# Other orders and buffer homes at eleven places of a hybrid decoder block

## The chip, the cores and the metric

The kernel runs on one core of a Trainium2 chip. A core has five engines that work side by side, each with its own stream of instructions: TensorE (PE, matrix products, with PEld for its weight loads), VectorE (DVE), ScalarE (ACT), GpSimd (POOL) and SyncE (SP), which here only issues transfers. Transfers run on 16 DMA engines, fed by the queues of the engines that issue them. Data lives in HBM (called DRAM tiles in the code), in SBUF, where the engines work, and in eight PSUM banks, into which PE accumulates. The metric is the device time of one execution in microseconds (us); lower is better.

## The reference, cut to what matters

One decoder block on a sequence of 1024 tokens with 1024 channels, in float32:

```python
mod = silu(c) @ w_ada + b_ada                       # six rows: shift, scale, gate, twice
h = rms_norm(x, pre_norm1_w) * (1 + sc1) + sh1
z, xbc, dt_raw, q, k, v, gates = split(h @ w_in)    # 1024, 1536, 16, 3 x 1024, 2048 columns
xbc = silu(causal_dwconv(xbc, 4 taps))              # Mamba-2 branch, 16 heads, chunks of 128
y_ssd = rms_norm(ssd(xbc, softplus(dt_raw + dt_bias), a_log, d_skip) * silu(z))
y_att = differential attention of q, k (rotary), v  # 8 pairs of heads, causal
merged = sigmoid(g_ssd) * (y_ssd @ w_ssd_o) + sigmoid(g_att) * (y_att @ w_attn_o)
x = x + g1 * rms_norm(merged @ w_out, post_norm1_w)
h2 = rms_norm(x, pre_norm2_w) * (1 + sc2) + sh2
u_gate, u_val = split(causal_dwconv(h2 @ w_up, 3 taps))      # 2 x 2816 channels
x = x + g2 * rms_norm((gelu(u_gate) * u_val) @ w_down, post_norm2_w)
```

## The kernel before, in words

**Products.** Nearly every product is made in three passes. An operand is split into a high part, rounded to `fp32r`, and a low part, the rest (`split`, L92: an ACT copy, L93, and a DVE difference, L94); PE adds high by high, high by low and low by high (`mm3`, L115 to 117). So a weight block costs one load of 512 KB, one copy on ACT and one difference on DVE before PE can use it. The two products of the feed-forward part, `w_up` and `w_down`, are made by a Strassen-like scheme of seven products instead of eight, on sums and differences of quarter blocks.

**Homes.** SBUF outside the weight rings is cut into 43 slots of 4 KB a partition (`Slots`, L35). `get` takes the slot that was freed longest ago, `get_last` the one freed last, `put` gives slots back. A tile that takes a slot waits for the last user of its previous tile. The weight rings `wraw` (3 buffers), `whi` and `wlo` (4 each) turn by themselves.

**Order.** Each engine runs its own instructions in order. Inside `tc.manual_schedule(engines=...)` the engines named keep the order in which the code issues; elsewhere a planner sets each engine's order by its own estimate of costs. SP's stream matters too: a store that waits for its data holds up the loads issued behind it.

**Stages,** in the order of the program, with the lines that the change touches:
- *Modulation and `h`* (L137 to 322).
- *Projection to `xbc`* (L429 to 461): twelve blocks, only PE in written order. Each block is followed by a convolution on ACT and DVE in `cu` (L440 to 447; L445 is the tap that reads the bank) and by three or four steps of the remaining modulation rows: `ada_load` (512 KB into one of four `adas`), `ada_sum` (DVE, L387), and once for eight of them `ada_row` (L389), with two matmuls (L398), two or three DVE operations and three small transfers. `down_sums(k)` (L411) makes the sums of quarter blocks of `w_down` that its seven products need: two loads into `wdr`, four subtractions in `wds` on POOL, two stores to `wtd` (L422), 11 rounds in all. Their homes are taken at L407 and L408.
- *z* (L478 to 498): three column groups of eight token blocks, six rounds of `down_sums` among them. Behind the loop stand the *decays* (L501 to 541): softplus and cumulative sums (L521, the matmuls at L523, the transposes L539 to `acT`) for the chunks.
- *Chunks of the SSD branch* (L543 to 765), with the `v` projection as filler for PE: `v_stream` (L596) yields after each contraction step; `split_v` (L583) puts four half operations for each weight tile in the background list `bg`, of which `run_bg` takes some at each turn.
- *Gates* (L769 to 779), the last five rounds of `down_sums`, *q and k* (L837 to 862: rotary positions, `store_qk` with 16 transfers a block, `load_y` and `turn_y` for the transposed `y`), *`w_ssd_o`* (L865 to 889; SP and PE in written order; `gths` at L869 and L876).
- *Attention* (L1114 to 1193): PE, DVE and ACT in written order; `probs` (L1044 to 1058) is the softmax of an item, `norm_o` (L1082) ends a group of rows, `att_split` (L1168) brings the result back as operands `oT`.
- *`w_attn_o`* (L1227 to 1250), by the planner: eight blocks `ao`, the split of the second half of `w_out` (`wo[1]`), and `early_sums` (L1211), four DVE sums (L1216 to 1219) on `w_up` for the first three up blocks.
- *Mix and norm* (L1391 to 1540): from here PE, DVE, ACT and POOL are in written order. `load_res` picks a pair of the banks m0 to m3 for each row block; `mix_square`, `mix_end` (L1415, `xr` scaled at L1427), `first_half`, `turn` (transposes L1452) make the feed-forward operand `HB`. `w_load` and `w_split` bring the up weights.
- *Up pairs* (L1542 to 1729): 22 of them, a gate block and a value block each; a pair takes seven steps of 12 matmuls (L1344 to 1346) into its banks X, Y and Z. Between steps the banks are copied to `evs` or added (L1712 and its neighbours), which I call passage copies. `w_ahead` splits the weights some steps on; `convs` says after which step the convolution, Gelu and product (`up_conv`, L1352) and the sums of the finished pair (`up_gsum`, L1375) are issued. Pairs 0 and 1 run together, in an order that is written out, and pair 2 starts it off into the loop.
- *Down* (L1731 to 1836): `left_part` loads the result back through two `gst` buffers (L1762) and splits it, `right_part` brings `w_down`; seven products (`downs`) of six double steps (11 contraction blocks) by four token blocks, 3 or 6 matmuls each (L1813 to 1815); then the norm and the output.

The down stage's homes (`gst`, and `gop` for two whole left operands, 24 tiles) are taken behind L1737, where the up stage gives its own back:

```python
1735    for n, _ in order:
1736        SL.put(*HB[n])
1737    SL.put(*sab, *hls, *cgv[0], *cgv[1], *evs, *ug, uv, *gsum)
```

Of the kernel before, what the change touches and what calls it, by code (L numbers as in the profile page):

```python
# [17 lines left out]
P = 128  # L18
# [43 lines left out]
def kernel(ctx: ExitStack, tc: tile.TileContext, a: dict, out: bass.AP, dbg=None):  # L62
# [398 lines left out]
    SL.put(*cu, *accr, *adas, nrow, brow)  # L461
    xsT, BT, CT = xbcT[:8], xbcT[8:10], xbcT[10:12]
# [14 lines left out]
    n_ev, n_dn = 0, 0  # L477
    for c0, wdt in ((0, 346), (346, 346), (692, 348)):  # L478
        wz = [load_moving(a["w_zdt"], 2 * kp, 2, c0, wdt, f"wz{c0}_{kp}") for kp in range(4)]
        for i in range(8):  # L480
# [16 lines left out]
            SP.dma_start(zd[i][:, c0 + lo - NH : c0 + lo - NH + n], e[:, 1, :n])  # L497
    SL.put(*ev, *wdr, *wds)


    CH = 8 * NH  # L501
    aexp = const("aexp", [P, NH])
    f = lambda t: t.rearrange("p c h -> p (c h)")
    t0 = f(sp0_)
    t1 = sp1_
    x_ = f(dtr)
    V.scalar_tensor_tensor(t0, x_, -1.0, x_, op0=ALU.mult, op1=ALU.min)
    A.activation(t0, t0, AF.Exp)
    V.tensor_scalar(t1, t0, 2.0, None, op0=ALU.add)
    V.reciprocal(t1, t1)  # L510
    V.tensor_tensor(t0, t0, t1, op=ALU.mult)
    V.tensor_tensor(t1, t0, t0, op=ALU.mult)
    dtf = f(dt)
    V.tensor_scalar(dtf, t1, 2.0 / 15, 2.0 / 13, op0=ALU.mult, op1=ALU.add)
    for m in (11, 9, 7, 5, 3, 1):
        V.tensor_tensor(dtf, dtf, t1, op=ALU.mult)
        V.tensor_scalar(dtf, dtf, 2.0 / m, None, op0=ALU.add)
    V.tensor_tensor(dtf, dtf, t0, op=ALU.mult)
    V.scalar_tensor_tensor(dtf, x_, 0.0, dtf, op0=ALU.max, op1=ALU.add)
    A.activation(aexp, rows[:, R_AL : R_AL + NH], AF.Exp)  # L520
    V.scalar_tensor_tensor(la, dt, -1.0, aexp[:, None, :].broadcast_to([P, 8, NH]), op0=ALU.mult, op1=ALU.mult)  # L521
    pa = ps_wa("acum_ps")
    T.matmul(pa[:, :CH], tri, f(la), start=True, stop=True)  # L523
    T.matmul(pa[:, CH : 2 * CH], ones, f(la), start=True, stop=True)
    V.tensor_copy(f(acum), pa[:, :CH])
    A.activation(f(ea), f(acum), AF.Exp)
    A.activation(f(cd), pa[:, CH : 2 * CH], AF.Exp)
    V.tensor_tensor(f(dte), pa[:, CH : 2 * CH], f(acum), op=ALU.subtract)
    A.activation(f(dte), f(dte), AF.Exp)
    hi_r = hi_t  # L530
    V.tensor_copy(hi_r, acum)
    V.tensor_copy(acx[:, :, :NH], hi_r.bitcast(F32))
    V.tensor_tensor(acx[:, :, NH:], acum, hi_r.bitcast(F32), op=ALU.subtract)
    acT = SL.get("acT", F32R, (P, S))
    V.memset(acT.bitcast(F32), 0.0)
    for half in range(2):
        pt = ps_wa(f"acT_ps{half}")
        for q in range(4):
            T.transpose(pt[:32, q * P : (q + 1) * P], acx[:, 4 * half + q, :], ident)  # L539
        V.tensor_copy(acT[:32, half * HALF : (half + 1) * HALF], pt[:32, :])  # L540
    SL.put(hi_t)
    dump("dt", dtf)
    dump("acum", f(acum))  # L543
# [39 lines left out]
    def split_v(vh, kp, raw):  # L583
# [7 lines left out]
        def low(k):  # L591
            return lambda: V.tensor_tensor(lo[:, k], raw[:, k], hi[:, k].bitcast(F32), op=ALU.subtract)
# [882 lines left out]
    with tc.manual_schedule(engines={EN.PE, EN.DVE, EN.Activation, EN.Pool}):  # L1475
# [114 lines left out]
        for m in range(2):  # L1590
            w_split(m, 4)
# [309 lines left out]
```

## Time and profile before

| | us |
|---|---|
| runs | 1933.61, 1944.59, 1941.97 |
| their median | 1941.97 |
| the profiled execution | 1938.42 |
| its span, first to last instruction | 1936.6 |
| PE busy in the span | 1871.4 (97%) |
| DVE busy | 1204.9 (62%) |
| ACT busy | 852.2 (44%) |
| POOL busy | 212.2 (11%) |
| mean granted TensorE clock | 0.994 of full speed |

How the rows shown below are read. A row such as `PE upx L1344 <- ACT evs L1712: 4.8, 2, 3.5` is one of the waits: instructions of PE at line 1344 with the tile `upx` stood 4.8 us in all, 2 times, the longest 3.5, for what ACT did to `evs` at line 1712. A row of windows begins with the stretch in us from the start of the span, then its length, and the busy time and number of instructions of PE, PEld, DVE, ACT and POOL, and ends with the granted clock, the share of DMA busy time and GB/s. A row of the timeline is start, duration, engine, line, operation, out<-in with shapes, count, and in square brackets the idle time before it and what ended it. A row of a group (line, engine, operation, tiles) has busy time and mean ns after the first bar, and the engine's idle time in front of it, with what ended it, after the second. A row of transfers has queue, number, size and the median us from issue to landing.

### The profile page before, as it was taken

The page shows a single profiled execution, that of the slowest core. Times are in us where ns is not written, and L with a number is a line of the kernel's source. Part 1 is how long each engine was busy: PE and PEld are TensorE (multiplying, and loading weights), DVE is VectorE, ACT ScalarE, POOL GpSimd, SP SyncE. Part 2 cuts the span into 40 slices and gives each one's busy share as a digit, 9 for nine tenths or more (in the row PEclk, how much of TensorE's full clock was granted, in tenths as well). Part 3 has the DMA queues.
Part 4 walks back from the last instruction along what each step waited for, and adds up shares of the span by engine and source line. Part 5 has one row for each costly group of instructions (what it writes and reads, how often), then busy time and mean ns, then how long its engine had stood idle before and what let it go on. Part 6 is the DMA issues. An engine that isn't in the chain of part 4 may idle for free.

```text
span 1936.6 us, 24512 instructions
## 1 busy us (share of the span) xinstructions
PE 1871.4 (97%) x9128; PEld 1557.7 (80%) x9128; DVE 1204.9 (62%) x1819; ACT 852.2 (44%) x1634; POOL 212.2 (11%) x214
## 2 busy tenths in 40 slices
PE   6999999999999999999999999999999999989998
PEld 4777898878887788888888787877788888878886
DVE  6968333565235227767766553367988888885545
ACT  5522224555223015665565522455554545455432
POOL 0253001453350000000000100000000000000001
PEclk9999999999999999999999999999999999999999
DMA  9876132233766646565651865122322322377754
GB/s 304 286 285 220 48 117 86 71 109 112 266 200 171 224 152 186 148 190 155 167 153 56 273 238 185 44 76 76 141 93 103 115 98 92 115 245 265 234 157 158
DMA packets 135821, 310.52 MB, mean 160 GB/s; under 512 B 16779, under 2 KB 48139, under 8 KB 135702
## 3 DMA queue, kind: packets, MB, share of 16 engines
q1 hardware_dynamic: 128406, 282.74, 45.6%
q0 software_dynamic: 7296, 26.22, 3.8%
q8 instruction: 72, 1.18, 0.3%
q14 instruction: 47, 0.39, 0.1%
HBM read 219.49 MB, written 89.41 MB: 160 GB/s over the span
## 4 chain that ended last, share of the span: by engine, by line
PE 78%; DVE 10%; DMA 5%; ACT 4%; issue 3%; SPq 1%; POOL 0%; POOLq 0%; DVEq 0%; ACTq 0%
PE upx L1345 3%; PE upx L1346 3%; PE upx L1344 3%; PE o L1078 3%; PE dx L1814 2%; PE dx L1815 2%; PE dx L1813 2%; PE upy L1345 2%; PE upy L1346 2%; PE upy L1344 2%; PE v L606 2%; PE v L607 2%; PE dy L1815 2%; PE dy L1813 2%; PE z L116 2%
## 5 line engine op out<-in xcount | busy, mean ns | idle before, releaser
L1344 PE MATMUL upx<-t,wu_t 128*128 128x512 f32 x264 | 104.0, 394 | 4.8 <-ACT evs L1712 4.8
L1345 PE MATMUL upx<-t,wu_t 128*128 128x512 f32 x264 | 103.7, 393 | 1.9 <-DVE t L1459 1.9
L1346 PE MATMUL upx<-t,wu_t 128*128 128x512 f32 x264 | 103.2, 391 | 0.0
L1066 ACT COPY aT<-at 128x512 f32<-128x512 f32 (+2 forms) x96 | 46.1, 480 | 110.0 <-PE at L1065 110.0
L1318 ACT ACTIVATE wu_t<-sab 128x512 fp32r<-128x512 f32 x57 | 34.0, 626 | 122.5 <-DVE sab L1335 122.5
L94 DVE TENSOR_TENSOR g_lo<-gst,g_hi 128x1024 fp32r<-128x1024 f32 (+1 forms) x42 | 47.5, 1134 | 56.9 <-ACT g_hi L93 56.9
L1078 PEld LDWEIGHTS o<-vt,aT 128*128 128x128 f32 x576 | 75.1, 192 | 9.5 <-ACT aT L1066 5.3
L1078 PE MATMUL o<-vt,aT 128*128 128x128 f32 x576 | 81.0, 277 | 0.2
L142 POOL TENSOR_TENSOR rsf<-rsf,nhalf 128x1 f32<-128x1 f32 x8 | 5.6, 703 | 639.6 <-DVE rsf L141 636.9
L93 ACT ACTIVATE g_hi<-gst 128x1024 fp32r<-128x1024 f32 (+1 forms) x42 | 41.5, 989 | 77.3 <-DMA gst<-gld_s 36.6
L115 PE MATMUL xbc<-hT,wx_hi 128*128 128x512 f32 x160 | 64.4, 402 | 4.8 <-DVE cu L445 4.8
L1039 DVE TENSOR_REDUCE nmx<-sc 128x1 f32<-128x640 f32 (+3 forms) x64 | 65.6, 1025 | 2.2
L142 POOL TENSOR_TENSOR sqt<-sqt,nhalf 128x4 f32<-128x4 f32 x16 | 16.2, 1010 | 443.3 <-DVE sqt L141 443.3
L1019 PE MATMUL sc<-kst,qst 128*128 128x512 f32 (+2 forms) x192 | 63.7, 340 | 0.0
L1344 PEld LDWEIGHTS upx<-t,wu_t 128*128 128x128 f32 x264 | 49.9, 189 | 16.6 <-ACT evs L1712 5.6
L1020 PE MATMUL sc<-klo,qst 128*128 128x512 f32 (+2 forms) x192 | 63.2, 346 | 0.0
L116 PE MATMUL xbc<-hT,wx_hi 128*128 128x512 f32 x160 | 63.0, 394 | 0.0
L117 PE MATMUL xbc<-hT,wx_lo 128*128 128x512 f32 x160 | 62.8, 393 | 0.0
L115 PE MATMUL z<-wz_hi,hT 128*128 128x346 f32 (+1 forms) x192 | 61.8, 324 | 0.0
L116 PE MATMUL z<-wz_lo,hT 128*128 128x346 f32 (+1 forms) x192 | 61.8, 322 | 0.0
L117 PE MATMUL z<-wz_hi,hT 128*128 128x346 f32 (+1 forms) x192 | 61.5, 320 | 0.0
L1345 PEld LDWEIGHTS upx<-t,wu_t 128*128 128x128 f32 x264 | 50.0, 189 | 13.2 <-DVE t L1459 2.9
(444 smaller groups left out, 5858.8 us busy)
## 6 DMA issues: line engine op xcount, KB each, us to landing
adas<-in_w_ada SPq DMA_DIRECT2D x32, 512.0 KB, 5.3
wdr<-in_w_down POOLq DMA_DIRECT2D x22, 512.0 KB, 7.2
wtd<-wds POOLq DMA_DIRECT2D x22, 512.0 KB, 4.7
wuf<-in_w_up SPq DMA_DIRECT2D x22, 512.0 KB, 3.5
gld_s<-gsum SPq DMA_DIRECT2D x22, 512.0 KB, 2.9
gst<-gld_s SPq DMA_DIRECT2D x20, 512.0 KB, 5.0
wdt_raw<-wtd SPq DMA_DIRECT2D x20, 512.0 KB, 4.6
wuv<-in_w_up SPq DMA_DIRECT2D x19, 512.0 KB, 3.9
```

Of the source, the lines that this page charges most:

```text
L115: T.matmul(ps, lh, rh, start=(i == 0), stop=False)
L116: T.matmul(ps, lh, rl, start=False, stop=False)
L117: T.matmul(ps, ll, rh, start=False, stop=(i == n - 1))
L1019: T.matmul(sc[:, n0:n1], qs_[s][:, tsl], ks_[s][:, n0:n1], start=True, stop=False)
L1020: T.matmul(sc[:, n0:n1], qs_[s][:, tsl], kl[s][:, n0:n1], start=False, stop=True)
L1039: V.reduce_max(nmx[:, bq, s : s + 1], sc[:, :L], axis=AX.X, negate=True)
L1078: T.matmul(po_of[j, grp][:, qi, :], at[:, k, :], vt[j % 2][:, kt, :], start=(kt == 0), stop=(kt == i))
L1344: T.matmul(out_, wh, xh_, start=(k == 0 and first), stop=False, skip_group_check=not first)
L1345: T.matmul(out_, wh, xl_, start=False, stop=False, skip_group_check=not first)
L1346: T.matmul(out_, wl, xh_, start=False, stop=(k == end), skip_group_check=not first)
L1813: T.matmul(bank[q], gh[:, kk, tsl], wh, start=(k == 0 and not more), stop=False, skip_group_check=more)
L1815: T.matmul(bank[q], gl[:, kk, tsl], wh, start=False, stop=(k == KF - 1), skip_group_check=more)
```

## The change

Eleven places are changed; no product is added or taken away.

1. *Projection.* In `ada_row` the three small transfers go out on POOL's queue instead of SP's. `wdr` and `wds` are taken after the block loop has given back `cu`, `accr`, `adas`, `nrow` and `brow`, instead of before it.
2. *Decays.* They become a function, issued after the first third of z. `acT` and `aexp` are taken before the z loop.
3. *`w_v`, second half.* Each tile is split by one ACT and one DVE operation that are issued in the stream itself, at steps 2 to 7 of its last block of the first half and 0 and 1 of the next.
4. *`y`.* `load_y(1)` goes from the head of the fifth q/k block to the fourth, before its `store_qk`. The first `gths` load comes inside the written order of SP.
5. *Attention.* POOL is added to the engines in written order.
6. *`w_attn_o`.* `early_sums` at blocks 1, 2 and 6 instead of 0, 1 and 6; the `wo[1]` tiles at 3 to 6 instead of 2 to 5.
7. *Mix.* Row blocks 0 and 1 use the banks wa, wb and wc instead of m0 to m3.
8. *First up weights.* `w_split(0, 1)` and one `w_load` are issued in row block 6 instead of 7, `w_split(1, 0)` in 7 instead of 6.
9. *Pairs 0 to 2.* High parts are issued before passage copies at several places; `high("t1", 0)` two steps up; `w_split(m, 5)` in two pieces; the copy of X of pair 2 later.
10. *The tables of the loop.* Convolutions of pairs 0 and 2 and the sums of pair 1 are issued one step later or split over two steps; at p = 3 and 4 of pair 2 they follow the passage copies and weight splits; at p = 2 the bank sum of pair 2 comes right after the first two.
11. *Down.* `left_part`, `right_part`, the matmuls (`down_mms`) and the first product come into the written order. In the last pair the operands' slots are given back as they are used, `gst` is taken at p = 3, and `left_part(0, ...)` is issued from p = 3 on, `right_part` from p = 5 on. Convolution, Gelu and sums of the last pair (`rest`) are issued within the first product, one group after each double step. `gop` takes its slots one by one; `es` takes them before `evs`, `ug` and the like are given back, `fo` after.

```diff
@@ ada_row
-        SP.dma_start(br, a["b_ada"][0:1, g * D : (g + 1) * D])
+        G.dma_start(br, a["b_ada"][0:1, g * D : (g + 1) * D])
         if g != 3:
-            SP.dma_start(nr, a["norms"][r : r + 1, :])
+            G.dma_start(nr, a["norms"][r : r + 1, :])
...
-        SP.dma_start(rowd[r], br)
+        G.dma_start(rowd[r], br)
     brow = SL.get("brow")
-    wdr = [SL.get_last(f"wdr{i}", F32, (P, 2, HALF)) for i in range(2)]
-    wds = [SL.get_last(f"wds{i}", F32, (P, 2, HALF)) for i in range(2)]
...
     SL.put(*cu, *accr, *adas, nrow, brow)
+    wdr = [SL.get_last(f"wdr{i}", F32, (P, 2, HALF)) for i in range(2)]
+    wds = [SL.get_last(f"wds{i}", F32, (P, 2, HALF)) for i in range(2)]
@@ z; decays() holds what stood behind the loop
+        if c0 == 0:
+            decays()
@@ split_v, v_stream
-        later(("wv", vh, kp), high(0), high(1), low(0), low(1))
+        if vh == 0:
+            later(("wv", vh, kp), high(0), high(1), low(0), low(1))
+            return
+        finished.add(("wv", vh, kp))
+        A.activation(hi, raw, AF.Copy)
+        return lambda: V.tensor_tensor(lo, raw, hi.bitcast(F32), op=ALU.subtract)
...
-                    if vh == 0 and i == 7 and k % 2 == 1:
-                        split_v(1, k // 2, v_raw.pop(0))
-                        if k == 1:
-                            v_raw.append(fetch_v(1, 3))
+                    if (vh == 0 and i == 7 and k > 1) or (vh == 1 and i == 0 and k < 2):
+                        if k % 2 == 0:
+                            v_low.append(split_v(1, (k // 2 - 1) % 4, v_raw.pop(0)))
+                        else:
+                            v_low.pop()()
+                            if k == 3:
+                                v_raw.append(fetch_v(1, 3))
@@ q and k, w_ssd_o
-            load_y(1)
...
+            if n == 3:
+                load_y(1)
...
-    SP.dma_start(gths[0], gsd[0])
     with tc.manual_schedule(engines={EN.SP, EN.PE}):
+        SP.dma_start(gths[0], gsd[0])
@@ attention, w_attn_o
-    with tc.manual_schedule(engines={mybir.EngineType.PE, mybir.EngineType.DVE, mybir.EngineType.Activation}):
+    with tc.manual_schedule(engines={EN.PE, EN.DVE, EN.Activation, EN.Pool}):
...
-        if j in (0, 1, 6):
-            early_sums(j if j < 2 else 2)
-        if 2 <= j < 6:
-            kp = j - 2
+        if j in (1, 2, 6):
+            early_sums(min(j - 1, 2))
+        if 3 <= j < 7:
+            kp = j - 3
@@ mix and norm
-        pms[i] = [ps_m(2 * (i % 2) + ch, f"mix{i}_{ch}") for ch in range(2)]
+        if i < 2:
+            pms[i] = [(ps_wa, (ps_wb, ps_wc)[i])[ch](f"mix{i}_{ch}") for ch in range(2)]
+        else:
+            pms[i] = [ps_m(2 * (i % 2) + ch, f"mix{i}_{ch}") for ch in range(2)]
...
                     w_split(0, 0)
-                    w_split(1, 0)
-                if i == 7 and n == 1:
                     w_split(0, 1)
                     w_load()
+                if i == 7 and n == 1:
+                    w_split(1, 0)
                     w_split(1, 1)
@@ pairs 0 to 2 (the highs of t3 and b22, w_split(m, 5) move likewise)
+        high("t1", 0, r1s)
         t2_sum(3)
...
-            if k == 1:
-                for m in range(2):
-                    A.copy(ev_of(m, 1), banks[m]["X"])
...
+        t3_sum(3)
+        SL.put(*r1s)
+        for m in range(2):
+            A.copy(ev_of(m, 1), banks[m]["X"])
+        high("t3", 0, hb1)
...
         up_mms(2, 0)
-        A.copy(ev_of(2, 0), banks[2]["X"])
...
             high("t4", k, hb2)
+        A.copy(ev_of(2, 0), banks[2]["X"])
@@ tables
-            (2, 2): ((0, 0), (0, 1)),
+            (2, 2): (),
...
-            (3, 2): ((2, 0),),
-            (3, 3): ((2, 1),),
-            (3, 4): ((2, 2),),
+            (3, 2): (),
+            (3, 3): ((2, 0),),
+            (3, 4): ((2, 1), (2, 2)),
...
-        convs[3, 1] = [(up_gsum, 1, i) for i in range(4)]
+        convs[3, 1] = [(up_gsum, 1, i) for i in range(2)]
+        convs[3, 2] = [(up_gsum, 1, i) for i in range(2, 4)]
...
-                if m == 2 and p in (3, 4):
-                    for f_, *x_ in todo:
-                        f_(*x_)
-                    todo = []
...
-                    if m > 2:
-                        V.tensor_tensor(cg[:, :HALF], bank["Z"], ev_of(m, 0), op=ALU.add)
+                    if m == 2:
+                        up_conv(0, 0)
+                        up_conv(0, 1)
+                    V.tensor_tensor(cg[:, :HALF], bank["Z"], ev_of(m, 0), op=ALU.add)
...
-                    if m == 2:
-                        V.tensor_tensor(cg[:, :HALF], bank["Z"], ev_of(m, 0), op=ALU.add)
@@ last pair and down; left_part and right_part as before, but for gop's slots
+                if m == NPAIR - 1:
+                    SL.put(*HB[order[p][0]])
+                    if p == 3:
+                        SL.put(*sab)
+                        gst = [SL.get_last(f"gst{i}", F32, (P, 2, HALF)) for i in range(2)]
+                    if p >= 3:
+                        left_part(0, p - 3)
+                    if p >= 5:
+                        wd[p - 5] = right_part(0, p - 5)
...
+        rest = [[(up_conv, m, 0), (up_conv, m, 1)], [(up_conv, m, 2), (up_conv, m, 3)], [(up_conv, m, 4), (up_gsum, m, 0), (up_gsum, m, 1)], [(up_gsum, m, 2), (up_gsum, m, 3)]]
+        for kp in range(KP):
+            for q in range(4):
+                down_mms(0, kp, q)
+                if q == 0 and kp + 4 < KP:
+                    left_part(0, kp + 4)
+                elif q == 1 and kp + 2 < KP:
+                    wd[kp + 2] = right_part(0, kp + 2)
+                elif q == 2:
+                    if kp < KP - 1:
+                        left_part(1, kp)
+                    for f_, *x_ in rest[kp] if kp < len(rest) else ():
+                        f_(*x_)
+        left_part(1, KP - 1)
+    es = [SL.get(f"es{i}", F32, (P, 2, HALF)) for i in range(4)]
+    SL.put(*cgv[0], *cgv[1], *evs, *ug, uv, *gsum)
...
-    for kp in range(KP):
-        left_part(0, kp)
```

More of the change, by code (lines that the diff above doesn't have):

```diff
@@ L1595 @@
             both(3, [k])
+        cgv = [[SL.get(f"c{n}{i}") for n in ("g", "v")] for i in range(2)]
+        for k in range(KH):
+            HB["b22"][k] = new_hl(f"b22_{k}")
         for k in range(KH):
@@ L1598 @@
             both(4, [k])
-        cgv = [[SL.get(f"c{n}{i}") for n in ("g", "v")] for i in range(2)]
+        for m in range(2):
+            w_high(m, 5)
+        for k in range(KH):
+            high("b22", k, c22)
         for m in range(2):
@@ new lines, in down_mms @@
+        def down_mms(p, kp, q):
+            rn, bk = downs[p][1:]
+            more = rn in ("t2", "t3", "t4", "b22")
+            o = dbank[bk][q]
+            tsl = slice(q * P, (q + 1) * P)
+            gh, gl = gop[p % 2][kp]
+            for kk in range(min(2, KF - 2 * kp)):
+                k = 2 * kp + kk
+                wh, wl = wd[kp][0][:, kk, :], wd[kp][1][:, kk, :]
+                T.matmul(o, gh[:, kk, tsl], wh, start=(k == 0 and not more), stop=False, skip_group_check=more)
+                T.matmul(o, gh[:, kk, tsl], wl, start=False, stop=False, skip_group_check=more)
+                T.matmul(o, gl[:, kk, tsl], wh, start=False, stop=(k == KF - 1), skip_group_check=more)
@@ L1655, in w_ahead @@
+        wd = {}
         def w_ahead(m, p):
```

211 lines of the change are left out of this document (97 added, 114 removed).

## The prediction, made before the changed kernel ran

> **What bounds the kernel now.** I read the page first: busy time by engine, and the chain that ended last.
>
> ```profile
> PE 1871.4 (97%) x9128; PEld 1557.7 (80%) x9128; DVE 1204.9 (62%) x1819; ACT 852.2 (44%) x1634; POOL 212.2 (11%) x214
> PE 78%; DVE 10%; DMA 5%; ACT 4%; issue 3%; SPq 1%; POOL 0%; POOLq 0%; DVEq 0%; ACTq 0%
> ```
>
> TensorE is the bound nearly everywhere, and the change removes no matmul. It can gain only where PE stands still or runs slowly. So I cut the span into windows. The first number of a row is the window's length, the second PE's busy time, and the granted clock stands before the last two.
>
> ```profile
> 100.00:120.00 20.00, 18.83 (x83) 15.31 (x82) 13.53 (x10) 4.94 (x5) 10.29 (x11) 1.00 0.91 346
> 178.00:200.00 22.00, 18.35 (x71) 14.01 (x70) 14.12 (x14) 5.76 (x6) 0.00 (x0) 0.92 0.19 41
> 314.00:330.00 16.00, 13.02 (x73) 10.82 (x71) 9.25 (x18) 9.13 (x26) 4.29 (x4) 0.89 0.57 191
> 405.00:415.00 10.00, 7.92 (x39) 5.59 (x38) 6.90 (x9) 5.92 (x15) 4.95 (x4) 1.00 0.58 161
> 613.00:650.00 37.00, 34.56 (x166) 27.50 (x165) 10.84 (x14) 8.10 (x11) 0.00 (x0) 1.00 0.62 207
> 1069.00:1077.00 8.00, 5.88 (x28) 4.74 (x27) 4.02 (x8) 2.94 (x5) 2.00 (x4) 0.79 0.94 316
> 1093.00:1110.00 17.00, 14.77 (x58) 10.02 (x58) 9.57 (x13) 8.40 (x13) 0.00 (x0) 1.00 0.90 305
> 1184.00:1190.00 6.00, 4.53 (x20) 3.49 (x19) 4.82 (x7) 2.29 (x3) 0.00 (x0) 1.00 0.87 300
> 1262.00:1290.00 28.00, 26.56 (x128) 21.73 (x127) 17.29 (x29) 15.54 (x34) 3.09 (x5) 1.00 0.36 130
> 1290.00:1330.00 40.00, 37.65 (x169) 29.80 (x168) 30.05 (x49) 21.25 (x39) 0.00 (x0) 1.00 0.15 47
> 1330.00:1365.00 35.00, 30.22 (x126) 24.21 (x125) 30.00 (x37) 21.18 (x29) 0.00 (x0) 0.95 0.36 122
> 1682.08:1712.00 29.92, 29.92 (x134) 24.77 (x132) 27.00 (x34) 17.36 (x24) 0.00 (x0) 1.00 0.58 187
> 1712.00:1740.00 28.00, 22.92 (x92) 18.25 (x91) 19.85 (x20) 12.91 (x14) 0.00 (x0) 0.88 0.78 259
> ```
>
> The row from 1682.08 is the steady up stage: 11 steps, no idle time, 2.72 us a step. Each of the other rows loses length less busy time, and (1 - clock) times the length on top where the clock fell. In order: 1.2; 3.65 + 1.8 = 5.4; 3.0 + 1.8 = 4.7; 2.1; 2.4; 2.1 + 1.7 = 3.8; 2.2; 1.5; 1.4; 2.35; 4.8 + 1.75 = 6.5. The last row has 5.1 idle and 3.4 of lost clock; part of the slow clock falls within the wait, so I count 7.1. The sum is 41 us. That is nearly all the change can win. What each place waits for (engine, total us, times, longest):
>
> ```profile
> PE dx L1814 <- DVE wdb_lo L94: 5.1, 1, 5.1
> PE xbc L115 <- DVE cu L445: 4.8, 2, 3.6
> PE upx L1344 <- ACT evs L1712: 4.8, 2, 3.5
> PE acT_ps L539 <- DVE sm L533: 2.5, 1, 2.5
> PE at L1065 <- DVE sqt L1087: 2.1, 1, 2.1
> PE v L607 <- DVE wv_lo L592: 2.1, 1, 2.1
> PE mix L1402 <- DVE mt L1244: 1.5, 1, 1.5
> PE h2tr L1452 <- DVE xr L1427: 1.2, 1, 1.2
> ```
>
> **The clock behind a wait.** The waits of 2.5 and 2.1 us at 314 and 1069 are followed by a lower clock (0.89, 0.79), the 2.1 us at 405 is not (1.00). A long wait is thus paid again, about 1.7 us, and removing it wins both. [...]
>
> **The change, part by part.** Everything is us saved, with both bounds.
>
> *Projection stage (rows' transfers to POOL's queue, homes of the `w_down` sums).* The buffers `wdr` and `wds` now take the slots of `brow`, `nrow` and two `adas`, so no `down_sums` can start before the last `ada_row`. Now they run beside the xbc blocks.
>
> ```profile
> 175.06 1.29 DVE L387 SCALAR_TENSOR_TENSOR accr<-adas,scl,accr 128x1024 f32<-128x1024 f32 x1 [3.02 <-DMA adas<-in_w_ada]
> 90.33 1.11 POOL L422 DMA_DIRECT2D wtd<-wds  x2
> 166.94 1.12 POOL L422 DMA_DIRECT2D wtd<-wds  x2
> L398 PE MATMUL adar<-accr,ones x16: 591/592/592, 132.7 to 221.0; 128*128 128x512 f32 x16
> ```
>
> Before the 3.6 us stall DVE itself waits 3.0 for an `adas` load, and the convolution PE needs is queued behind. Six rounds of four 512 KB transfers leave this stretch, 12.6 MB in the some 90 us around those rows, or 140 GB/s, against 346 in flight in the first row of the windows (their last number is GB/s); that should shorten the load. The three small transfers of a row also leave SP's queue, where a store waiting for DVE blocks the weight loads behind it. On POOL's queue they stand ahead of the sums, in the order of the program. But the order of DVE here is the planner's. Of 5.4 + 1.2 = 6.6 I take 4.4; bounds -2 and 6.6. The moved rounds start at about 221 and take (166.94 - 90.33)/5 = 15.3 each, six end at about 313, just as the chunk stage begins: free, but only just.
>
> *Decays within z.*
>
> ```profile
> 262.67 0.29 DVE L521 SCALAR_TENSOR_TENSOR sm<-sm,aexp 128x128 f32<-128x128 f32 x1
> 313.34 0.38 PE L523 MATMUL acum_ps<-sm,tri 128*128 128x128 f32 x2
> ```
>
> The DVE chain is already done at 263, and PE's part comes 50 us later, followed by 2.5 us of waiting for the copies. Issued after the first third of z, the copies hide behind z matmuls. If the planner sets the two PE pieces too early, each can wait as long as now (2.5), so bounds -0.3 and 4.7; I take 3.7, one us left for such a wait.
>
> *Second half of `w_v`* is split by whole tiles right in the stream instead of in four quarters through the background list. The list is what makes `wv_lo` late (2.1). The order here is written out, so 2.0; bounds 1 and 2.1. *`y` loads and first gate load:*
>
> ```profile
> 610.37 1.80 SPq L815 DMA_DIRECT2D yr<-yd  x4
> 627.04 0.33 SPq L876 DMA_DIRECT2D gth<-gsd  x1
> 627.54 0.32 SPq L869 DMA_DIRECT2D gth<-gsd  x1
> ```
>
> The `yr` loads stood behind sixteen `store_qk` transfers; they go ahead of them and delay these by 1.8, which nobody waits for so early. The load of L869 (block 0) went out after that of block 1; in SP's written order it cannot, so `mout` of block 0 no longer comes last. 2.2 of 2.4; bounds 0.5 and 2.4.
>
> *Attention's end and `w_attn_o` (early sums one block later, POOL in the written order).*
>
> ```profile
> 1067.65 0.69 DVE L1216 TENSOR_TENSOR ws<-ws 128x512 f32<-128x512 f32 x1
> ```
>
> Four such sums (2.8 us) stand on DVE between the softmax operations of the last item, and PE waits 2.1 for it. One block later they fall behind it, if the planner does not hoist them again: 2.5 of 3.8, bounds -1 and 3.8. The 2.2 at 1093, waits for `oT` splits fed by loads at a DMA share of 0.90, gets less traffic ahead of it: 1.0, bounds -2 and 2.2. POOL pinned alone: nothing, its `pow` is hidden by fills of PE. *Mix blocks 0 and 1 in banks nobody holds:* the whole 1.5 goes, as `mT[7]` is needed only 21 matmuls later: 1.4, bounds 0.5 and 1.5.
>
> *Early `w_split(0, 1)` and load.*
>
> ```profile
> 1278.83 1.16 ACT L1318 ACTIVATE wu_t<-wus 128x512 fp32r<-128x512 f32 x2 [3.52 <-DMA wus<-wsd]
> ```
>
> ACT waits 3.5 for this load with the last `mix_square` queued behind it. Issued one row earlier it has landed; the chain to `h2tr` moves up by more than the 1.4 PE loses. 1.4, bounds 0.9 and 1.4.
>
> *First up pairs.*
>
> ```profile
> 1337.14 1.06 ACT L1364 ACTIVATE ug<-ug 128x1024 f32<-128x1024 f32 x1
> 1338.11 0.57 ACT L1712 COPY evs<-upx 128x512 f32<-128x512 f32 x1
> 1359.18 1.24 ACT L1361 ACTIVATE ug<-cg,vec 128x1024 f32<-128x1024 f32 x1 [2.17 <-DVE gsum L1380]
> ```
>
> PE goes on only when the copy at 1338.11 is done (two such waits, 4.8 in all, the longer 3.5); the copy stands behind a Gelu. In the new order it stands ahead. At 1359 it stands behind an operation that waits for four `gsum`; these are split two and two and that operation is moved a step on. The copies at L1582 and L1621 move behind the highs PE needs next. Of 2.35 + 6.5 = 8.9 I take 8.0; the Gelu is now ahead of the copy of Y, which may cost up to 1. Bounds 6 and 8.9.
>
> *Down operands in the last pair.* Each left part is a load into one of two `gst` buffers, a copy on ACT and a difference on DVE:
>
> ```profile
> gst<-gld_s SPq DMA_DIRECT2D x20, 512.0 KB, 5.0
> L93 ACT ACTIVATE g_hi<-gst 128x1024 fp32r<-128x1024 f32 (+1 forms) x42 | 41.5, 989 | 77.3 <-DMA gst<-gld_s 36.6
> L94 DVE TENSOR_TENSOR g_lo<-gst,g_hi 128x1024 fp32r<-128x1024 f32 (+1 forms) x42 | 47.5, 1134 | 56.9 <-ACT g_hi L93 56.9
> ```
>
> A buffer turns in 5.0 + 1.0 + 1.1 = 7.1. The first is free 1.4 after step 2 starts (after the difference of step 5's weights): landed at 6.4, copied at 7.4, and the passage copy of Y behind it on ACT is done at 8.0, just inside the 3 x 2.72 = 8.2 when PE needs it. Part 2 uses that buffer again: landed at about 13.6, the very end of the pair (5 x 2.72), and the first right part stands behind it on ACT and DVE. So **PE will wait some 2 us for the first `wdb_lo`**, where it now waits 5.1 in the second operand. 5.0 of 7.1; bounds 1 (3 us, then the slow clock) and 7. Afterwards the same two buffers deliver a part per 3.6 us against 5.4 us of PE per operand: enough.
>
> Sum: 4.4 + 3.7 + 2.0 + 2.2 + 2.5 + 1.0 + 1.4 + 1.4 + 8.0 + 5.0 = 31.6. I take 2 off for waits that the planner sets elsewhere in the stretches it orders: **30 us**. The profiled execution took 1938.42 (span 1936.6), so 1908.4; the runs' median, 1941.97, lies 3.6 above it. I say 1910, between the two.
>
> **Rivals.**
> - *Only the written orders pay.* Where the planner orders DVE (projection, z, y, attention's end) a wait returns in another place. Left: 2.0 + 1.4 + 1.4 + 8.0 + 5.0 = 17.8, so 1922. For: those five stretches have no pinned DVE; against: four of their waits have one visible cause that goes.
> - *All waits go*, the 41: 1897 to 1901. Against: the `gst` chain above.
> - *The waits only change their owner.* The down operands start no earlier, since their two buffers set the pace and left parts now stand ahead of copies PE needs each step, and the orders outside lose what others win: 4 to 6 net, about 1936. Against: the copy behind the Gelu is too plain.
> - *Slower: POOL is late.* Six rounds pushed behind 221. The slots they hold are homes of the chunk stage (`M`, `prev`, `tt`), first needed at about 321 (an estimate: the decays' matmuls at 313.34 and some 8 us of the first chunk's own). They are late above (321 - 221)/6 = 16.7 us a round (15.3 now; below 14 with the DMAs idler would be my estimate from the 0.19 share at 178). Each further us costs six; from 23 a round the loss passes the 30 and 10 more, at 26 the time is 1965.
>
> **Numbers.** Forecast 0.55 (own range 1900 to 1919), only written orders 0.22, all waits 0.08, owners change 0.10, POOL late 0.05. A difference below 0.5% (9.7 us) can't be told from none. Faster 0.55 + 0.22 + 0.08 = 0.85, same 0.10, slower 0.05. The range 1894 to 1932 holds the first three.
>
> **What would show it.** PE's waits for `evs`, `mt`, `xr` and `acT_ps` gone; POOL idle from 70 to 210 and busy to the chunk stage; a wait of about 2 us at the first `dx` in place of 5.1 at the second; granted clock 1.00 around the places at 1069 and 1338. I am wrong if the sum of PE's idle time falls by less than 15, or if PE waits at the first chunks for something POOL wrote.

## The result, and the profile after

The changed kernel took 1927.16 us (median of six runs, 1924.19 to 1931.72), the kernel before 1940.12 in the runs beside it (1933.61 to 1944.59). The ratio is 0.9938, 95% interval [0.9914, 0.9963]: faster by 13 us, not by the 30 forecast. The time lies inside the range of 1894 to 1932, but outside the forecast's own, 1900 to 1919. The profiled execution of the changed kernel took 1931.72 (span 1929.6), the slowest of its six; a second profile of the same kernel has a span of 1925.3.

PE is still the bound, as the busy times and the chain that ended last show:

```profile
PE 1868.5 (97%) x9128; PEld 1556.7 (81%) x9128; DVE 1203.8 (62%) x1815; ACT 852.9 (44%) x1630; POOL 214.0 (11%) x225
PE 82%; DVE 6%; DMA 5%; ACT 4%; issue 2%; SPq 1%; POOL 0%; POOLq 0%; ACTq 0%; DVEq 0%
```

The windows of the changed kernel (length, busy time of PE, PEld, DVE, ACT and POOL, granted clock, DMA share, GB/s):

```profile
90.00:125.00 35.00, 35.00 (x157) 28.97 (x156) 19.97 (x17) 8.85 (x9) 0.00 (x0) 1.00 0.48 171
170.00:212.00 42.00, 42.00 (x183) 34.11 (x182) 24.59 (x23) 10.25 (x11) 1.45 (x3) 1.00 0.19 49
240.00:256.00 16.00, 12.18 (x67) 11.89 (x67) 8.69 (x13) 5.62 (x8) 8.59 (x11) 0.90 0.72 242
280.00:296.00 16.00, 10.35 (x55) 9.87 (x54) 5.42 (x6) 4.41 (x7) 9.21 (x11) 0.82 0.76 255
336.00:500.00 164.00, 164.00 (x898) 133.26 (x898) 100.43 (x140) 87.06 (x228) 74.59 (x62) 1.00 0.32 111
1064.00:1078.00 14.00, 10.17 (x67) 8.49 (x66) 8.54 (x15) 5.62 (x10) 2.27 (x4) 1.00 0.71 239
1078.00:1112.00 34.00, 28.86 (x115) 21.30 (x114) 15.70 (x26) 15.98 (x31) 3.57 (x5) 0.91 0.75 250
1175.00:1190.00 15.00, 15.00 (x68) 12.43 (x67) 4.83 (x7) 2.30 (x3) 0.00 (x0) 1.00 0.62 223
1280.00:1330.00 50.00, 49.78 (x236) 41.25 (x236) 37.56 (x62) 27.08 (x50) 1.47 (x2) 1.00 0.24 79
1330.00:1370.00 40.00, 36.44 (x156) 28.55 (x155) 36.78 (x46) 23.62 (x33) 0.00 (x0) 1.00 0.32 112
```

In these windows the projection, the chunk stage from 336 on, the mix and, but for 0.2 us, the start of the up pairs now run without a gap. But z, in which PE had waited for no weights before, loses 3.8 and 5.7 us in two windows of 16 and some clock on top (0.90, 0.82); attention's end loses 3.8 in 14 and the head of `w_attn_o` 5.1 in 34. What PE waits for, in the same profile (engine, total us, times, longest):

```profile
PE z L115 <- ACT wz_hi L93: 9.5, 2, 5.6
PE ao L115 <- ACT oT L93: 4.2, 4, 2.4
PE at L1077 <- DVE sqt L1099: 3.5, 1, 3.5
PE upx L1356 <- DVE cv L1789: 3.0, 3, 1.4
PE pb L676 <- ACT M L680: 1.6, 1, 1.6
PE upy L1356 <- ACT evs L1786: 1.2, 3, 0.6
PE dx L1720 <- DVE wdb_lo L94: 0.9, 1, 0.9
```

The old waits for `cu`, `wv_lo`, `mt`, `xr` and the copies of `acT_ps` are gone, that for `wdb_lo` is down from 5.1 to 0.9. The waits for `wz_hi`, `M` and `cv` are new, those for `sqt` and `oT` are longer.

Cut at the first and last matmul of each stage (the starts in the trace, as in these rows of the views of the tiles `z` and `v`, first of before, then of after), the time splits as in the table.

```profile
L115 PE MATMUL z<-wz_hi,hT x192: 316/321/720, 221.0 to 312.9; 128*128 128x346 f32 x128, 128*128 128x348 f32 x64
L608 PE MATMUL v<-wv_hi,hT x128: 387/393/628, 319.7 to 489.6; 128*128 128x512 f32 x128
```

```profile
L115 PE MATMUL z<-wz_hi,hT x192: 315/321/720, 214.1 to 321.7; 128*128 128x346 f32 x128, 128*128 128x348 f32 x64
L616 PE MATMUL v<-wv_hi,hT x128: 387/393/398, 323.4 to 491.7; 128*128 128x512 f32 x128
```

| stage, us | before | changed | changed, second profile | second less before | forecast |
|---|---|---|---|---|---|
| projection (first `xbc` of L115 to first z) | 133.25 | 126.27 | 126.27 | -7.0 | -4.4 |
| first z to last v (decays, `w_v`) | 268.55 | 277.65 | 275.27 | +6.7 | -5.7 |
| `w_ssd_o` | 93.99 | 91.52 | 91.35 | -2.6 | -2.2 |
| last score to last `ao` | 120.17 | 126.14 | 122.96 | +2.8 | -3.5 |
| last `ao` to last mix | 93.08 | 91.36 | 91.38 | -1.7 | -1.4 |
| first up to end of pair 4 (`h2tr`, first pairs) | 111.02 | 104.41 | 104.37 | -6.7 | -9.4 |
| pair 5 to second down product | 361.09 | 356.82 | 357.86 | -3.2 | -5.0 |
| span | 1936.6 | 1929.6 | 1925.3 | -11.3 | -30 (with 2 held back) |

The stretches between these rows differ by less than 0.5 us each. Five rows have the sign of the forecast and lie within 2.7 us of it. The loss is in two rows, z and the end of attention, which have the other sign.

### The profile page after: what moved, and what is told of

It is laid out like the page before. It is cut to its first block, busy times and chain, and to the rows that moved or that the text cites. A ratio compares the mean times of both kernels' runs of the same rounds, so it can differ in the third digit from the quotient of the medians.

```text
span 1929.6 us, 24511 instructions
## 1 busy us (share of the span) xinstructions
PE 1868.5 (97%) x9128; PEld 1556.7 (81%) x9128; DVE 1203.8 (62%) x1815; ACT 852.9 (44%) x1630; POOL 214.0 (11%) x225
## 4 chain that ended last, share of the span: by engine, by line
PE 82%; DVE 6%; DMA 5%; ACT 4%; issue 2%; SPq 1%; POOL 0%; POOLq 0%; ACTq 0%; DVEq 0%
PE upx L1357 4%; PE upx L1358 4%; PE upx L1356 4%; PE o L1090 3%; PE dx L1720 2%; PE dx L1721 2%; PE dx L1719 2%; PE xbc L117 2%; PE xbc L116 2%; PE xbc L115 2%; PE upy L1357 2%; PE upy L1356 2%; PE upy L1358 2%; PE dy L1721 2%; PE dy L1720 2%; PE dy L1719 2%
## 5 line engine op out<-in xcount | busy, mean ns | idle before, releaser
L115 PE MATMUL z<-wz_hi,hT 128*128 128x346 f32 (+1 forms) x192 | 63.7, 334 | 9.9 <-ACT wz_hi L93 9.5
L115 PE MATMUL xbc<-hT,wx_hi 128*128 128x512 f32 x160 | 63.5, 397 | 0.0
L1356 PEld LDWEIGHTS upx<-t,wu_t 128*128 128x128 f32 x264 | 49.6, 188 | 15.4 <-DVE cv L1789 4.3
L1374 DVE SCALAR_TENSOR_TENSOR ug<-cg,vec,ug 128x1023 f32<-128x1023 f32 (+1 forms) x44 | 56.3, 1280 | 6.3 <-ACT ug L1373 5.1
```

What stands on the lines that cost most here:

```text
L115: T.matmul(ps, lh, rh, start=(i == 0), stop=False)
L1356: T.matmul(out_, wh, xh_, start=(k == 0 and first), stop=False, skip_group_check=not first)
```

## The experiments

All are edits of the changed kernel unless said; each was timed against the kernel before on the same chip. No run undoes the places 3, 4 and 7 to 11; what these gave is read from the stretches and the waits.

**Homes alone undone.**

```diff
     brow = SL.get("brow")
+    wdr = [SL.get_last(...)]; wds = [SL.get_last(...)]
...
     SL.put(*cu, *accr, *adas, nrow, brow)
-    wdr = [SL.get_last(...)]; wds = [SL.get_last(...)]
```

> The changed kernel with the homes of the w_down sums taken before the block loop again, so that they run beside the projection and not beside z. From the first z matmul to the last of v the changed kernel takes 277.6 us (268.6 before), the projection 126.3 (133.3 before). Theory traffic: PE's waits for wz_hi (9.5 us, and the lower clock behind them) come from the sums' transfers, which share the DMA engines with the fourth z weight tile; then these waits are under 1.5 us, z to v takes 262 to 265, the projection 130 to 134, and the time falls by 6 to 10 us from 1927. Theory decays: the waits come from the decays issued inside z; then z to v stays at 276 to 279, the projection gives back 5 to 7, and the time rises to about 1933.

Measured: 1933.97 us, ratio 0.9972 [0.9959, 0.9984]. z to v took 263.5, and PE's waits for `wz_hi` were gone: so far the traffic theory. But the projection took 141.9, worse than before the change, and the time rose. DVE's and POOL's timelines of this kernel show why:

```profile
172.96 0.49 POOL L392 DMA_DIRECT2D brow<-in_b_ada  x1 [3.09 <-DMA rowd<-brow]
```

```profile
174.88 0.68 DVE L399 TENSOR_TENSOR brow<-adar,brow 1x512 f32<-1x512 f32 x1 [10.35 <-DMA brow<-in_b_ada]
```

The load of a row stands on POOL's queue behind the sums' rounds; DVE waits 10.35 us for it with the convolution queued behind, and PE waits 8.4 for `cu`. The two edits of the projection need each other: rows on POOL's queue are free only when no sums run there.

**Decays behind z again** (`decays()` after the loop).

> The changed kernel with the decays behind the z loop again. Theory traffic: PE still waits some 9.5 us for wz_hi in z, and the wait for the acT_ps copies (2.5 us) is back at the end of z, so z to v takes 278 to 282 and the time is 1927 to 1931. Theory decays: the waits for wz_hi fall under 2 us, z to v takes 266 to 270, and the time falls to about 1917.

Measured: 1926.07 us, 0.9933 [0.9916, 0.9950], like the changed kernel (1926 to 1927). The wait for `wz_hi` stays (3.9 us, once) and the wait of 2.5 us for `acT_ps` is back, yet z to v takes 273.1, not the 278 to 282 expected, against 272.6 to 277.7 in the kernels with the decays inside z. So the traffic theory holds in the waits, but the decays' move, forecast at 3.7, brought nothing here. (The profiled execution of this kernel took 1931.05, its other four 1925.37 to 1926.30: in it PE waited 4.3 us for `yT` between `v` and `w_ssd_o`; in the other profiles such a wait is at most 0.7.) The price of the move came out in a later experiment.

**Early sums at their old blocks** (`early_sums` at 0, 1, 6; `wo[1]` at 2 to 5), and **POOL out of the written order of attention**.

> The changed kernel with early_sums at blocks 0, 1 and 6 and the wo[1] tiles at 2 to 5 again. From the last score matmul to the last of w_attn_o the changed kernel takes 126.1 us (120.2 before). Theory hoist: with the sums one block later the planner puts the split of block 1 as well as the four sums into the last softmax, and the ring of raw buffers holds SP longer; then this stretch returns to 119.5 to 121.5 and the time to about 1921. Theory POOL: the written order of POOL puts the pow of the last norm behind the stores of the sums; then the stretch stays at 125 to 127 and the time at 1927.

> The changed kernel with POOL out of the written order of attention. Theory hoist: the stretch from the last score matmul to the last of w_attn_o stays at 125 to 127 us and the time at 1925 to 1929. Theory POOL: the stretch falls to 119.5 to 121.5 and the time to about 1921.

Measured: 1923.45 us, 0.9914 [0.9896, 0.9933], and 1925.25, 0.9934 [0.9914, 0.9955]. The stretch from the last score to the last `ao` is 121.1 with the old blocks, 124.1 with POOL free: the cause is the position of the sums and of the `wo[1]` tiles, and POOL's order plays no part that shows. DVE's timeline of the changed kernel has the last softmax between these rows:

```profile
1062.81 1.22 DVE L94 TENSOR_TENSOR wao_lo<-wao_raw,wao_hi 128x1024 fp32r<-128x1024 f32 x1
...
1064.15 1.22 DVE L94 TENSOR_TENSOR wao_lo<-wao_raw,wao_hi 128x1024 fp32r<-128x1024 f32 x1
1065.28 1.22 DVE L1051 TENSOR_REDUCE nmx<-sc 128x1 f32<-128x1024 f32 x1
...
1070.19 0.69 DVE L1228 TENSOR_TENSOR ws<-ws 128x512 f32<-128x512 f32 x1 [1.63 <-DMA ws<-in_w_up]
...
1070.92 0.69 DVE L1229 TENSOR_TENSOR ws<-ws,ws 128x512 f32<-128x512 f32 x1
1071.53 0.21 DVE L1068 SCALAR_TENSOR_TENSOR coef<-ssum,nlam,rsm 128x1 f32<-128x1 f32 x1
1071.66 0.69 DVE L1230 TENSOR_TENSOR ws<-ws,ws 128x512 f32<-128x512 f32 x1
```

The planner fills the gaps that it sees in the written order with whatever comes next in the program. One block later, that is the split of block 1 (1.22 us, ahead of the row maximum that the softmax needs) and still the sums, which now wait 1.63 for their load in the middle of the softmax. PE's wait for `sqt` goes with them: 3.1 to 3.5 us in the profiles with the sums at the new blocks, 2.1 with the old ones, where the sums still stand in the softmax but that split does not.

**The changed kernel again.**

> The changed kernel itself once more, to see what a second profile of it shows: from the first z matmul to the last of v 272 to 278 us, from the last score matmul to the last of w_attn_o 122.5 to 126.5, the time 1924 to 1930. If the 126.1 of its first profile were its rule, it would come back; in three kernels that leave this stretch alone it was 122.9 to 124.1.

Measured: 1926.09 us, 0.9938 [0.9923, 0.9952]; z to v 275.3, last score to last `ao` 123.0. Over seven profiles of kernels with the sums where the changed one has them, this last stretch takes 122.9 to 126.1. PE's waits for `oT`, high and low part, are 5.2 us in the first profile of the changed kernel and 3.2 in the second; what sets them from one execution to the next is not shown.

**Both projection edits undone** (rows on SP's queue, homes before the block loop).

> The changed kernel with both edits of the projection undone: rows on SP's queue, homes of the w_down sums as before. Theory traffic (the sums cost PE more beside z than beside the projection): projection 132 to 134 us (126.3 in the changed kernel), z to v 262 to 265 (272.6 to 277.7), the time 1920 to 1925, under the changed kernel. Rival (the waits in z belong to the decays or come and go by chance, and the projection's edits are a gain): z to v 270 or more, the time 1930 or more. It also says whether the 8.4 us wait of the kernel with the homes alone undone came from the rows on POOL's queue: then it is gone, and the longest wait for cu is 3 to 4.

Measured: 1925.69 us, 0.9930 [0.9914, 0.9946]. The projection takes 131.9, z to v 267.1, no wait for `wz_hi`, and the longest wait for `cu` is 3.3. In the trace the two stages together take 399.0 against 401.5 and 403.9 in the changed kernel; in the time there is no difference that could be told. **The first of the eleven places, forecast at 4.4 us, is worth nothing on balance.** That it fell short of 1920 to 1925 has a reason in z to v, 3.5 above the 263.5 of the first experiment: a wait of 1.9 us for `M` in the first chunk, with 6.8 us at half clock behind it.

**A home of its own for the fourth z tile.** A column group needs four weight tiles, and three raw buffers hold the loads; the fourth is issued only when the group changes.

```diff
+    wzr = SL.get("wzr")
...
-        wz = [load_moving(a["w_zdt"], 2 * kp, 2, c0, wdt, ...) for kp in range(4)]
+        wz = [load_moving(a["w_zdt"], 2 * kp, 2, c0, wdt, ...) for kp in range(3)]
+        raw = wzr[:, : 2 * wdt].rearrange("p (k c) -> p k c", k=2)
+        SP.dma_start(raw, ...)   # rows 6 P to 8 P, then the split as before
```

> The changed kernel with a home of its own for the fourth z weight tile, so that its load does not wait for one of three raw buffers at the change of the column group; the sums stay beside z. Theory late issue (the load is issued when it is nearly due and the sums' transfers then double its time): PE's waits for wz_hi fall under 1 us, z to v is 263 to 267, the projection 126.3, the time 1914 to 1919. Rival (the DMA engines are simply short in z): z to v stays over 272 and the time at 1925 to 1929.

Measured: 1923.11 us, 0.9922 [0.9908, 0.9936]. How long the fourth tile's load takes can be read from the transfers around a change of group (size, median us from issue to landing): first of before at the second change, at 282 us; then of the changed kernel at the first, at 244, with the sums' transfers, and at the second, at 284.

```profile
wz_raw<-in_w_zdt SPq DMA_DIRECT2D x1, 348.0 KB, 3.1
```

```profile
wtd<-wds POOLq DMA_DIRECT2D x2, 512.0 KB, 4.3
wdr<-in_w_down POOLq DMA_DIRECT2D x2, 512.0 KB, 7.7
wz_raw<-in_w_zdt SPq DMA_DIRECT2D x1, 346.0 KB, 7.9
```

```profile
wz_raw<-in_w_zdt SPq DMA_DIRECT2D x1, 348.0 KB, 7.8
```

3.1 us without the sums, 7.9 and 7.8 beside them. With the load issued a group earlier PE no longer waits for `wz_hi`, with all the traffic still there: the next three loads of `wz_raw` still take 7.8 to 8.6 us at the first change, and nobody waits for them. In the second profile of the changed kernel the load at the second change took 2.9 us, and PE waited for `wz_hi` once instead of twice: how often a load meets the sums' transfers changes from one execution to the next. But z to v fell only to 269.7, and the time missed its 1914 to 1919, since the next late thing took over, PE's wait for the decays' DVE chain, with a record of 3.41 us at half clock behind it:

```profile
PE acum_ps L505 <- DVE sm L503: 3.4, 1, 3.4
```

In the changed kernel the wait for `wz_hi` had covered this one to 0.6.

**Besides, early sums at blocks 4, 5 and 6.**

```diff
-        if j in (1, 2, 6):
-            early_sums(min(j - 1, 2))
-        if 3 <= j < 7:
-            kp = j - 3
+        if j in (4, 5, 6):
+            early_sums(j - 4)
+        if 2 <= j < 6:
+            kp = j - 2
```

> The kernel with the own home of the fourth z tile, and besides early_sums at blocks 4, 5 and 6 and the wo[1] tiles at 2 to 5. Theory hoist: with no sums near the last softmax and no ring buffer held by their stores, the stretch from the last score matmul to the last of w_attn_o falls from 123 to 126 to 117 to 121, and the time to 1909 to 1915. Rival: the planner hoists the splits of blocks 1 and 2 there instead and the oT loads stay late; the stretch stays at 122 or more.

Measured: 1918.39 us, 0.9889 [0.9873, 0.9906], 4.7 below the kernel without this edit. The stretch takes 119.6 against 124.4; no sums stand in the last softmax, and PE's wait for `sqt` is 1.0 us. The total missed its expectation because it was built on a z stage of 263 to 267.

**Besides, the decays in two pieces:** the DVE chain behind the first column group as it was, everything from the matmuls of `acum_ps` on behind the second.

> The kernel with the own home of the fourth z tile and the late early_sums, and besides the decays in two pieces: the DVE chain behind the first column group as in the changed kernel, everything from the two matmuls on (acum_ps) behind the second. Theory chain: PE's wait of 3.5 us at acum_ps, and the half clock behind it, came from a DVE chain that PE's order meets some 17 us after its start, held up by stores of ev and by POOL; 30 us later it is long done. Then z to v falls from 269.7 and 271.3 to 263 to 267 and the time from 1918.4 to 1911 to 1915. Rival: the wait moves to the first chunk (px or pb), z to v stays at 269 or more and the time at 1917 to 1920.

Measured: 1913.79 us, 0.9861 [0.9845, 0.9877]; z to v 266.0. The wait at `acum_ps` is gone, so it came from the chain: PE met its 21 DVE operations too early. (The 17 us of the expectation is about right for the changed kernel, 16 from the chain's start to PE's arrival; with the home for the fourth tile PE arrived after 9 us, and the chain took 12.5.) What held the chain up can be read, but was not tested: POOL's subtractions (last section), and an eviction in the middle of it that waited for a store:

```profile
256.41 0.52 DVE L545 SCALAR_TENSOR_TENSOR ev<-ev,z 128x346 f32<-128x346 f32 x1 [1.92 <-DMA zd<-ev]
```

The row is of the kernel with the home for the fourth tile alone. A wait in the first chunk stays, for the product at L674 (`cbm` in the code, in the trace part of `sm`), with 3.41 us at half clock behind it, so the 3.7 of the decays are not all there yet:

```profile
PE px L669 <- DVE sm L674: 2.1, 1, 2.1
```

**Besides, one step's delay more in the tables** of the first pairs (the product of pair 0, the first and third operation of pair 2).

> The kernel before this one in the list, with one more step's delay in the tables: the product of pair 0 from step 4 to 5 of pair 2, the first operation of pair 2 from step 3 to 4 of pair 3 and its third from 4 to 5. Theory DVE queue: PE's waits for cv (1.1 and 1.6 us) and evs (0.5 and 0.8) in the first pairs come from convolutions that stand ahead of the passage sums on DVE; with some 1.25 us of them moved behind, the stretch from the first up matmul to the end of pair 4 falls from 104.4 to 101.5 to 103.3. Rival (DVE is simply full there): the waits turn up at the next steps and the stretch stays at 104 or more.

Measured: 1912.42 us, 0.9854 [0.9838, 0.9871], no different from the kernel before it. From the first up matmul to the end of pair 4 it takes 104.4 as it did, and DVE's busy time there explains it (window of this kernel):

```profile
1318.00:1366.00 48.00, 44.43 (x192) 35.24 (x192) 44.89 (x56) 26.35 (x37) 0.00 (x0) 1.00 0.31 110
```

DVE is busy for 44.89 of 48 us, more than PE. The waits for `cv` changed their step, not their sum. DVE has little room left here: the rival, that it is simply full, held.

## Why the prediction was wrong

The sign was right, and the time lies in the range of 1894 to 1932. The size was not right: 13 us in the medians and 11.3 between spans of profiles, against 30. By the prediction's own sign of being wrong, a sum of PE's idle time that falls by less than 15, it was wrong too: from 65.2 us (span less busy time) it fell to 61.1 and 56.6 in the two profiles. Of its other signs, the waits it named went, POOL had no sums until 217 and then until 298, and the clock at 1069 was full in the first profile but not in the second. By its steps:

- **Projection (4.4) and "free, but only just".** This step failed. The stall went as argued, even 7.0 of it. The error is in the cover: the six moved rounds were costed at nothing as long as POOL finished before the chunk stage. POOL did finish, rounds of 13 us from 217.6 to 298.2, well ahead of the 313 of the prediction. What it missed is that z's fourth weight tile is loaded just when it is due, and its load takes 7.8 to 7.9 us instead of 3.1 beside the sums. The prediction used the argument "less traffic shortens the load" for the stage that the rounds leave, and did not ask it of the stage that they enter. Kernels without the move show the exchange: 131.9 + 267.1 against 126.3 + 275.3 to 277.7. So the term of 4.4 became a loss of 2.5 to 4.9 us in the traces, and nothing that the times show.
- **Decays (3.7) and `w_v` (2.0).** `wv_lo` is gone from the waits. With the sums away from z the stage took 263.5 in one profile, 5.0 less than before against the 5.7 forecast, and 267.1 in the other, where a 1.9 us wait for `M` was followed by 6.8 us at half clock. So the removal came as argued, but the decays' wait partly changed its place: where before had 2.5 us at `acT_ps`, each of the ten profiles with the decays inside z has 1.4 to 2.3 in the first chunk (`M` or `px`), in six of them with half clock behind. What the prediction allowed for a wait set by the planner (1 us) was too little, and beside the sums the wait at `acum_ps` alone is 3.4 to 3.5 once nothing else covers it. No run separates the 2.0 of `w_v` from the rest of the row.
- **`y` and gates (2.2):** 2.5 and 2.6. Right.
- **Attention's end (2.5) and `w_attn_o` (1.0).** Wrong in sign: the stretch lost 2.8 to 6.0. The prediction named the condition, "if the planner does not hoist them again", and took the wrong side of it; the first profile lies beyond the sum of its bounds, -3. The planner hoisted both the sums and the split in front of them; with the sums at blocks 4 to 6 the wait for `sqt` is 1.0 and the stretch 119.6, so the step that failed here is the new position.
- **Mix (1.4):** 1.7. Right.
- **`h2tr` and first pairs (1.4 + 8.0):** 6.7. The waits behind the Gelu and behind four `gsum` are gone and with them the half clock (0.95 in the 35 us from 1330 before, 1.00 in 40 now). The 2.7 that lack lie in the new waits for `cv` and `evs`, 0.3 to 1.4 us each and 3.3 in all; the prediction looked for orders and made nothing of DVE's busy time, which its own row at 1330 gave as 30.00 of 35 us, and which is 36.78 of 40 in the changed kernel.
- **Down operands (5.0):** 4.3 and 3.2 in the two profiles. The wait for the first operand is there: in the second profile 1.1 us for the high part and 1.0 for the low, together the predicted 2; in the first 0.2 and 0.9. Not foreseen were two short waits in the last pair (0.4 and 0.6 in the second profile), where the left parts now share ACT and DVE with the passage copies.
- **The sum.** In the second profile z and attention account for 12.4 + 6.3 of the shortfall, the first pairs and the down operands for 2.7 + 1.8; projection, gates and mix gave 3.3 more than forecast, and the 2 held back were far too few. Of z's 12.4, 8.2 go when the rounds leave z (275.3 against 267.1); the other 4.2 stay in that kernel and are 0.7 in the one with the homes alone undone, where no half clock followed the first chunk's wait.

Of the rivals, "only the written orders pay" came nearest, and nearly by its own division: places in written order gave 1.7 + 6.7 + 3.2 = 11.6, while the stretches that the planner orders gave 7.0 - 6.7 + 2.6 - 2.8 = 0.1 (with `w_v`, which the rival counts as written, in the second of these). It was priced at 1922 and had a chance of 0.22; it deserved the first place. "POOL late" suspected the right move, the rounds behind 221, but for the wrong reason: POOL was done at 298, and it was their transfers that cost.

## What to carry to other kernels

When a transfer-heavy step is moved, look in the stage that it enters for the load with the least slack (here the one tile more than there are buffers) and price that load at the slower rate (7.8 to 7.9 us here, against 3.1); a stage without a single wait may stand one late load away from many. An edit in a stretch that a planner orders should be forecast at zero until it is known what the planner will put into the place that becomes free, while an edit in a written order is worth what the trace shows. Waits hide one another: behind `wz_hi` lay the decays' chain, and with both repaired, and the sums out of the softmax, the change came to 0.9861 of the kernel before.

## What the runs showed of the hardware

**Half clock behind a wait depends on more than its length.** The prediction took a long wait to be paid again. In the changed kernel PE idled 3.8 us of the window at 1064 quoted above, 3.5 of them in one wait, with the clock at 1.00. In its second profile a wait of 3.1 us at the same place was followed by one record of 3.41 us at half clock, and so was a wait of 2.1 in the kernel with the early sums at their old blocks. The rows are of the latter:

```profile
PE at L1077 <- DVE sqt L1099: 2.1, 1, 2.1
```

```profile
1064.00:1076.00 12.00, 9.87 (x60) 8.44 (x58) 6.79 (x11) 5.65 (x10) 2.27 (x4) 0.86 0.81 275
```

In the first chunk, of the ten profiles with the decays inside z, the four with a wait of 1.4 to 1.7 us have no lower clock behind it, and the six with 1.9 to 2.3 all have one, for 3.41 or 6.83 us: 1.00 in the 11 us from 319 of the changed kernel, which waited 1.6, and 0.83 in the 10 us from 312 with the decays in two pieces, which waited 2.1. In the traces of before and of the changed kernel each record of the lower clock is at 0.50 and, but for the last of each trace, 3.41 or 6.83 us long. What decides whether a wait has one behind it is not shown. For a forecast of this kernel I take from it a chance, not a certainty, of losing 1.7 or 3.4 us (half of 3.41 or 6.83) behind each wait of 1.9 to 3.5 us: an estimate from the waits named here.

**Beside POOL's subtractions short DVE operations took longer.** But for one reciprocal (0.95 us), the DVE operations of 128x128 in the decays take 0.23 to 0.31 us in the changed kernel when POOL does not compute; while POOL's subtractions run (253.30 to 257.2) each takes 1.2 or more:

```profile
253.30 1.36 POOL L416 TENSOR_TENSOR wds<-wdr,wds 128x512 f32<-128x512 f32 x1 [2.06 <-DMA wdr<-in_w_down]
254.62 1.33 POOL L417 TENSOR_TENSOR wds<-wdr,wdr 128x512 f32<-128x512 f32 x1
255.91 1.34 POOL L418 TENSOR_TENSOR wds<-wdr,wds 128x512 f32<-128x512 f32 x1
```

```profile
253.44 1.36 DVE L492 TENSOR_TENSOR sm<-sm,sm 128x128 f32<-128x128 f32 x1
254.84 1.25 DVE L493 TENSOR_TENSOR sm<-sm 128x128 f32<-128x128 f32 x1
256.13 1.20 DVE L495 TENSOR_SCALAR sm<-sm 128x128 f32<-128x128 f32 x1
257.36 0.29 DVE L497 TENSOR_TENSOR sm<-sm,sm 128x128 f32<-128x128 f32 x1
```

Each of the three ends within 0.15 us after a POOL instruction, and the next one, after POOL's last, takes 0.29 again. Not every DVE operation did so: the evictions into `ev` (128x346) that began at 269.36 and 280.70, while POOL computed, took 0.52 us, as did the one at 273.10 without it. What makes the difference is not shown. If POOL's subtractions are the cause, the moved sums also lengthened the decays' chain, by some 3 us (an estimate: the three rows less 0.27 each). That this shifted PE's wait at `acum_ps` was not tested by itself.
